# Quarter-sized second-projection operands and earlier requests for kept products in a two-layer hybrid trunk

## The chip, the cores and the metric

The kernel runs on one core of a Trainium2 chip, in one launch. The metric is the device time of that launch in microseconds (us). The kernel before has been run three times: 2802.8, 2805.24 and 2806.19 us, median 2805.24 us. One more execution, of 2806.7 us, was recorded by the profiler; its trace has a span of 2804.9 us, so 1.8 us of that execution lie outside the span.

## The reference

One step of a decoder trunk with two layers is computed for a prompt of 1024 tokens and eight single-token samples, width 1024. Each layer is a token mixer (a gated linear recurrence with a short convolution in layer 0, a state-space mixer in layer 1) and then a squared-ReLU MLP:

```
h = rmsnorm(x, norm_mlp[l]) * (1.0 + s2) + sh2
x = x + g2 * (jnp.square(jax.nn.relu(h @ mlp_w1[l])) @ mlp_w2[l])
```

`mlp_w1` is 1024 x 4096 and `mlp_w2` is 4096 x 1024. Shift, scale and gate (`sh2`, `s2`, `g2`) come from a projection of a condition vector (the "ada" weights). The change lies in these two MLPs alone. Mixers, states and the final norm are computed as before.

## The kernel before

**Layout.** Activations lie transposed: features on the 128 partitions, 1032 columns (1024 tokens and 8 samples) in two halves of 516 (`HX`). Each fp32 value is split into a high part (`fp32r`, a ScalarE cast) and a low part (what is left, a VectorE subtraction), and each product is made of three matmuls, high x high, high x low, low x high (`mm3`, L487; the matmuls are L490, L493 and L494).

**Two-by-two block products.** Both projections are computed block-wise with seven products in place of eight (a fast matrix multiplication scheme), so sums and differences of blocks are formed of weights, inputs and results.

**First projection** (the loop over `AOPS`, L865). The 32 tiles of hidden features make 16 pairs `p`. For each pair there are seven products `q`; each is 24 matmuls of 258 columns into one of four PSUM buffers `pd`. Products 1 and 2 of the first eight pairs (`LEAD`) and of the last four (`TAIL`, pairs 12 to 15) are computed ahead of the others, in a row. Product 1 of such a pair is spilled to DRAM (`keep`, L896) and so is the finished block of product 2 (`B`, L806). They are fetched again when the pair's product 6 comes: `kept` (L856) requests product 1 into half of a `t6` buffer (four of these; weight sums use them too), and L886 requests the block into its slot. Product 6 is evicted by L899, a VectorE subtraction that reads the fetched product 1. The order around the last pairs is: products 1 and 2 of pairs 12, 13, 14, 15, then 6, 7, 5, 4, 3 of pair 12, and so on.

**Between the projections.** Hidden blocks and their sums go to DRAM under seven names (`td`), each as two halves of eight pairs.

**Second projection** (the loop over `BOPS`, L939). Seven products `i`; each has eight steps `j`. A step takes one quarter `q` of the pairs (four pairs) and one half `mp` of the output tiles, 48 matmuls. In the first product the quarters come as 0, 1, 0, 1, 2, 3, 2, 3; in the others as 0, 1, 2, 3, 0, 1, 2, 3. In the last product the steps are halved by columns. After each step the weights of three steps on are prepared (`prepare`, L972): loads on SP's queue into two `raw` buffers and, for four of the products, a second load and a sum or difference in a `t6` buffer (L451, L453, L455), two of them with a store for later; then a cast (L456) and a subtraction (L457). While layer 0's second projection runs, the "ada" weights of layer 1 are loaded and multiplied between the steps (L308, L320).

**Operands of the second projection.** `load_op(i, kh)` (L833) fetches half `kh` of product `i`'s operand: it takes two buffers of one tag, one for the eight high parts and one for the eight low parts. It issues four DMAs of 516 KB on GpSimd's queue (`dma_aux`, L225, kept in program order) into the low buffer, and leaves a list of four parts, each a cast (L843) and a subtraction (L844) over two pairs. `split_op(n)` (L850) issues the next `n` parts. Three sets of two buffers rotate (`BSET`). From product 2 on, the second half of product i+1 is requested after step 5 and the first half of product i+2 after step 7 (L978 to L981), and the parts are issued after the steps by the list `(2, 1, 1, 1, 1, 1, 0, 1)`: of the four parts of a product's second half, one after step 7 of the product before it, two after its own step 0 and one after its step 1. Quarter 2 is first used in step 2 and quarter 3 in step 3.

**What sets the order.** Each engine works through its own list in order. A scheduler makes the lists from the program's order and priorities; instructions that are "kept in program order" stay in it on their engine. GpSimd does nothing but issue DMAs in these stages.

Of the kernel before, what the change touches and what calls it, by code (L numbers as in the profile page):

```python
# [161 lines left out]
def kernel(ctx: ExitStack, tc: tile.TileContext, A: dict):  # L162
# [62 lines left out]
    def dma_aux(out, in_):  # L225

        tc.keep_in_program_order(nc.gpsimd.dma_start(out=out, in_=in_))  # L227
# [557 lines left out]
    def mlp(l, gi, finish, more=None):  # L785
# [7 lines left out]
        def slot(p, i):  # L793
            s = (7 * p + i) % 8
            return M["X"][:, 4 + s // 2, s % 2 * HX:s % 2 * HX + HX]
# [34 lines left out]

        R, todo = {}, []

        def load_op(i, kh):  # L833

            pool, tag = ((big, M["tags"][0]), (ph.pool, "hr"), (big, M["tags"][1]))[BSET[i][kh]]
            ts = [pool.tile([P, KT * 520], F32R, name="rr", tag=tag, bufs=2) for _ in range(2)]
            hi, lo = R[i, kh] = [t[:, 0:KT * HX].rearrange("p (k t) -> p k t", t=HX) for t in ts]
            d = td[BOPND[BPROD[i]]][kh]

            def parts():  # L840
                for c in range(0, KT, 2):
                    src = lo[:, c:c + 2].bitcast(F32)
                    tc.keep_in_program_order(S.copy(hi[:, c:c + 2], src))  # L843
                    V.tensor_sub(lo[:, c:c + 2], src, hi[:, c:c + 2].bitcast(F32))  # L844
                    yield
            for c in range(0, KT, 2):
                dma_aux(lo[:, c:c + 2].bitcast(F32), d[:, c:c + 2])
            todo.append(parts())

# [15 lines left out]
        for i, (p, q) in enumerate(AOPS):  # L865
            n = APOS[p, q]
            while len(got) <= n // 2:
                got.append(need(f"a{l}", len(got), AHEAD - 1))
            if i == 0:
                bg.drain(hgen.pop(3, None))  # L870
                sg = bg.add(mlp_sums())
                bg.step(sg)
            elif i == 2 * LEAD:
                bg.drain(hgen.pop(2), sg)
                sg = bg.add(mlp_more_sums())
            elif i == 2 * LEAD + 4:
                bg.drain(sg)
            if i == 2 * LEAD - 4:
                kept(0)
                kept(1)  # L880
            if q == 6:
                kept(p)
                if p and p + 1 in keep:
                    kept(p + 1)
            if p in SPLIT and q == (5 if p < 2 else 6):
                dma_aux(slot(p, 1), B[p])  # L886
            w = 512 * (n % 2), got[n // 2]
            pt = pd()
            product(w, q, pt)
            pv = pt[:, :, 0:HX // 2]  # L890
            if q == 1:
                U[p, 1] = t2(HX)
                S.copy(v2(U[p, 1]), pv)
                if p in SPLIT:
                    keep[p] = dr.tile([P, HX], F32, name="kept", tag=f"kept{p}")
                    dma_aux(keep[p], U[p, 1])  # L896
            elif q == 6:
                U[p, 1], U[p, 2] = saved.pop(p, U[p, 1]), t2(HX)
                V.tensor_sub(v2(U[p, 2]), v2(U[p, 1]), pv)  # L899
            elif q == 7:  # L900
                U[p, 3] = t2(HX)
                V.tensor_add(v2(U[p, 3]), pv, v2(U[p, 2]))
            elif q == 5:
                c = t2(HX)
                V.tensor_add(v2(c), pv, v2(U[p, 3]))
                V.tensor_add(v2(U[p, 2]), pv, v2(U[p, 2]))
                ff_out(p, q, c, -1.0)
            elif q == 2:
                c = t2(HX) if p in SPLIT else U[p, 1]
                V.tensor_add(v2(c), pv, v2(U[p, 1]))  # L910
                ff_out(p, q, c, 1.0)
            elif q == 4:
                c = U[p, 3] if p < NPAIR - 1 else t2(HX)
                V.tensor_add(v2(c), pv, v2(U[p, 3]))
                ff_out(p, q, c, -1.0)
            else:
                V.tensor_add(v2(U[p, 2]), pv, v2(U[p, 2]))
                ff_out(p, q, U[p, 2], 1.0)
            if n % 2:
                prepare(wpos[0] - 1 + AHEAD)  # L920
            if (p, q) == FRONT[1][-1]:
                load_op(0, 0)
            elif p == NPAIR - 2 and q in (7, 5, 4, 3):
                split_op()
            if (p, q) == (NPAIR - 1, 5):
                split_op(4)
                load_op(0, 1)
            bg.tick(2)

        x = new_x()  # L930
        for m in range(KT):
            dma_aux(x[:, m, :], xd[:, m])
        load_op(1, 0)
        acc = tp.tile([P, KT, NS], F32, name="racc", tag="racc", bufs=2)
        V.memset(acc, 0.0)
        fin = finish()
# [2 lines left out]
        for n, (i, hb, q, mp) in enumerate(BOPS):  # L939
# [3 lines left out]
                ada[0] = more()  # L943
            elif i == 6 and hb == 0 and j == 0:
                ada_steps(99)
            rh, rl = R[i, q // 2]
            seq = BSEQ if i else BFIRST
            qs = [qq for qq, mm in seq if mm == mp]
            for m in (2 * mp, 2 * mp + 1):
                if q == qs[0]:  # L950
                    pts[m] = pd()
                pt = pts[m]
                for b in range(2) if hb is None else (hb,):
                    c = slice(b * hw, b * hw + hw)
                    mm3(pt[:, b, 0:hw], [(hi[:, o:o + P], lo[:, o:o + P], rh[:, k, c], rl[:, k, c])
                                         for k, o in ((q % 2 * 4 + k, 256 * k + m % 2 * P) for k in range(4))],
                        q == qs[0], q == qs[-1])
                if q == qs[-1]:
                    for o, th in BOUT[BPROD[i]]:
                        mt = 4 * o + m  # L960
                        gate = mod[:, gi + mt, 0:1]
                        if hb is None:
                            xv = v2(x[:, mt, th * HX:th * HX + HX])
                            V.scalar_tensor_tensor(xv, pt[:, :, 0:hw], gate, xv, op0=ALU.mult, op1=ALU.add)
                        else:
                            xv = x[:, mt, th * HX + hb * hw:th * HX + hb * hw + hw]
                            V.scalar_tensor_tensor(xv, pt[:, hb, 0:hw], gate, xv, op0=ALU.mult, op1=ALU.add)
                        if hb != 1:
                            sv = pt[:, 0, 0:4] if th else pt[:, 1, hw - 4:hw]
                            av = acc[:, mt, 4 * th:4 * th + 4]  # L970
                            V.tensor_add(av, sv, av)
            prepare(wpos[0] - 1 + AHEAD)  # L972

            if i == 0:
                split_op((0, 2, 2, 0, 1, 1, 2, 0)[j])
            else:
                split_op((2, 2, 1, 1, 1, 1, 0, 1)[j] if i == 1 else (2, 1, 1, 1, 1, 1, 0, 1)[j] if i < 6 else (2, 1, 0, 0, 0, 0, 0, 0)[j] if hb == 0 else 0)
            if j == (5 if i else 3) and i < 6:  # L978
                load_op(i + 1, 1)
            elif j == 7 and i < 5:  # L980
                load_op(i + 2, 0)  # L981

            if i == 6 and j == 7 and hb == 0:
                V.tensor_mul(acc, acc, mod[:, gi:gi + KT, 1:9])
# [1143 lines left out]
```

## Time and profile before

| | |
|---|---|
| median of 3 runs | 2805.24 us |
| profiled execution | 2806.7 us, span 2804.9 us |
| TensorE matmul busy | 2654.7 us (95%), 19442 matmuls |
| VectorE busy | 1983.5 us (71%) |
| ScalarE busy | 1485.0 us (53%) |
| GpSimd busy | 266.5 us (10%) |
| moved by DMA | 525.63 MB |
| mean granted TensorE clock | 0.977 |

The profile is a page on one execution: busy time per engine, a strip of forty time slices, DMA queues, the chain of waits that ended last, and groups of instructions by source line. Behind it stands the trace, which can be asked for waits (who waited for whom), for the instructions of one engine in order of time, and for tables over chosen windows. `out<-in` names the tiles that an instruction writes and reads, L844 is a source line, and a bracket at the end of a timeline row tells how long the engine was idle before it and what released it. Matmuls overlap in the trace, so the spacing of their starts tells the rate, not the busy time of one. The first MLP's two projections run from about 560 to 883 us and from 883 to 1260 us of the span, the second's from about 2120 to 2444 us and from 2444 to 2793 us.

### The profile page before, as it was taken

The page shows a single profiled execution, that of the slowest core. Times are in us where ns is not written, and L with a number is a line of the kernel's source. Part 1 is how long each engine was busy: PE and PEld are TensorE (multiplying, and loading weights), DVE is VectorE, ACT ScalarE, POOL GpSimd, SP SyncE. Part 2 cuts the span into 40 slices and gives each one's busy share as a digit, 9 for nine tenths or more (in the row PEclk, how much of TensorE's full clock was granted, in tenths as well). Part 3 has the DMA queues.
Part 4 walks back from the last instruction along what each step waited for, and adds up shares of the span by engine and source line. Part 5 has one row for each costly group of instructions (what it writes and reads, how often), then busy time and mean ns, then how long its engine had stood idle before and what let it go on. Part 6 is the DMA issues. An engine that isn't in the chain of part 4 may idle for free. (4 is left out here: it accounts for less than half of the span.)

```text
span 2804.9 us, 49250 instructions
## 1 busy us (share of the span) xinstructions
PE 2654.7 (95%) x19442; PEld 2443.9 (87%) x19442; DVE 1983.5 (71%) x3668; ACT 1485.0 (53%) x2409; POOL 266.5 (10%) x492
## 2 busy tenths in 40 slices
PE   6999999999999988998899999999999999999897
PEld 4889888899999977898789897787779999999897
DVE  5666544788757555775789788998778776756676
ACT  5785511464444322356687767878756445433234
POOL 0000000023223100000000000000001322311000
PEclk9999999999999999999899999999999999999998
DMA  8232333257468899834545745444435655779764
GB/s 300 69 107 71 105 121 113 88 191 242 168 204 312 328 334 353 321 129 115 142 148 144 184 122 155 132 132 124 117 105 172 223 184 181 264 284 372 266 214 156
DMA packets 199256, 525.63 MB, mean 187 GB/s; under 512 B 32688, under 2 KB 50736, under 8 KB 199024
## 3 DMA queue, kind: packets, MB, share of 16 engines
q1 hardware_dynamic: 150640, 355.25, 40.3%
q0 software_dynamic: 48384, 167.23, 16.2%
q8 instruction: 153, 2.51, 0.4%
q14 instruction: 79, 0.65, 0.1%
HBM read 408.59 MB, written 113.80 MB: 186 GB/s over the span
## 5 line engine op out<-in xcount | busy, mean ns | idle before, releaser
L490 PE MATMUL pg<-hh,whi 128*128 128x256 f32 (+2 forms) x1616 | 535.8, 332 | 13.5 <-ACT hh L592 6.2
L493 PE MATMUL pd<-rr,whi 128*128 128x258 f32 x1792 | 512.3, 286 | 25.1 <-DVE rr L844 24.9
L493 PE MATMUL pg<-hl,whi 128*128 128x256 f32 (+2 forms) x1616 | 522.8, 324 | 1.9 <-DVE hl L593 1.9
L494 PE MATMUL pg<-hh,wlo 128*128 128x256 f32 (+2 forms) x1616 | 522.0, 323 | 0.0
L490 PE MATMUL pd<-rr,whi 128*128 128x258 f32 x1792 | 513.4, 287 | 0.0
L494 PE MATMUL pd<-rr,wlo 128*128 128x258 f32 x1792 | 510.5, 285 | 1.5 <-DVE wlo L467 1.1
L467 DVE TENSOR_TENSOR wlo<-raw,whi 128x1024 fp32r<-128x1024 f32 x222 | 270.7, 1221 | 216.5 <-ACT whi L466 209.9
L466 ACT CAST whi<-raw 128x1024 fp32r<-128x1024 f32 x222 | 231.4, 1044 | 349.4 <-PE pg L493 192.0
L493 PEld LDWEIGHTS pd<-rr,whi 128*128 128x128 f32 x1792 | 343.6, 192 | 29.2 <-DVE rr L844 27.0
L490 PEld LDWEIGHTS pd<-rr,whi 128*128 128x128 f32 x1792 | 343.7, 192 | 19.0 <-issue 16.5
L490 PEld LDWEIGHTS pg<-hh,whi 128*128 128x128 f32 x1616 | 308.0, 191 | 50.0 <-issue 8.8
L494 PEld LDWEIGHTS pd<-rr,wlo 128*128 128x128 f32 x1792 | 344.0, 192 | 4.0 <-DVE wlo L467 1.8
L493 PEld LDWEIGHTS pg<-hl,whi 128*128 128x128 f32 x1616 | 308.1, 191 | 31.1 <-issue 5.8
L494 PEld LDWEIGHTS pg<-hh,wlo 128*128 128x128 f32 x1616 | 307.4, 190 | 24.4 <-issue 0.7
L490 PE MATMUL pd<-hh,whi 128*128 128x258 f32 x1024 | 293.9, 287 | 18.6 <-DVE t L899 12.6
L493 PE MATMUL pd<-hh,whi 128*128 128x258 f32 x1024 | 292.7, 286 | 0.8 <-DVE hh L695 0.8
L494 PE MATMUL pd<-hh,wlo 128*128 128x258 f32 x1024 | 291.1, 284 | 0.0
L490 PEld LDWEIGHTS pd<-hh,whi 128*128 128x128 f32 x1024 | 196.8, 192 | 21.0 <-issue 13.6
L456 ACT CAST whi<-t 128x1024 fp32r<-128x1024 f32 x64 | 67.0, 1047 | 274.8 <-PE pd L493 116.8
L493 PEld LDWEIGHTS pd<-hh,whi 128*128 128x128 f32 x1024 | 196.3, 192 | 1.9 <-DVE hh L695 1.4
L494 PEld LDWEIGHTS pd<-hh,wlo 128*128 128x128 f32 x1024 | 196.6, 192 | 0.0
L490 PE MATMUL pg<-ffh,whi 128*128 128x264 f32 (+2 forms) x544 | 176.8, 325 | 2.1 <-ACT bcz L1633 1.5
(335 smaller groups left out, 5813.9 us busy)
## 6 DMA issues: line engine op xcount, KB each, us to landing
raw<-W SPq DMA_DIRECT2D x375, 512.0 KB, 4.3
td<-x POOLq DMA_DIRECT2D x224, 258.0 KB, 3.6
rr<-td POOLq DMA_DIRECT2D x112, 516.0 KB, 8.1
t<-ada SPq DMA_DIRECT2D x192, 256.0 KB, 5.4
t<-W SPq DMA_DIRECT2D x32, 512.0 KB, 5.8
sd<-t SPq DMA_DIRECT2D x32, 512.0 KB, 5.8
t<-sd SPq DMA_DIRECT2D x32, 512.0 KB, 5.5
t<-csd SPq DMA_DIRECT2D x64, 256.0 KB, 4.6
```

Source lines behind the costliest of these rows:

```text
L456: S.copy(hi, h)
L466: S.copy(hi, raw)
L467: V.tensor_sub(lo, raw, hi.bitcast(F32))
L490: mm = PE.matmul(pt, wh, xh, start=first and i == 0, stop=False)
L493: PE.matmul(pt, wh, xl, start=False, stop=False)
L494: PE.matmul(pt, wl, xh, start=False, stop=last and i == n - 1)
```

## The change

The operand of a second-projection product comes in four quarters instead of two halves. A quarter takes one buffer, with its four high parts ahead and its four low parts behind; it is requested by two DMAs of 516 KB and has two parts. A buffer is free for the next quarter when that quarter's last step is done, so requests go out after steps 4, 5, 6 and 7 (in the first product after 2, 3, 6 and 7), one quarter each. The parts are issued by the list `(1, 1, 1, 1, 1, 1, 0, 2)` from product 2 on: both parts of quarter 2 after step 7 of the product before, the parts of quarter 3 after steps 0 and 1. The count of DMAs, their sizes, the casts, the subtractions and the matmuls stay as they are.

In the first projection, the kept products of pairs 12 and 13 and the block of pair 12 are requested ahead of product 1 of pair 15, two products ahead of product 6 of pair 12, where they were requested before.

```
-        def load_op(i, kh):
-
-            pool, tag = ((big, M["tags"][0]), (ph.pool, "hr"), (big, M["tags"][1]))[BSET[i][kh]]
-            ts = [pool.tile([P, KT * 520], F32R, name="rr", tag=tag, bufs=2) for _ in range(2)]
-            hi, lo = R[i, kh] = [t[:, 0:KT * HX].rearrange("p (k t) -> p k t", t=HX) for t in ts]
-            d = td[BOPND[BPROD[i]]][kh]
+        def load_op(i, q):
+
+            pool, tag = ((big, M["tags"][0]), (ph.pool, "hr"), (big, M["tags"][1]))[BSET[i][q // 2]]
+            t = pool.tile([P, KT * 520], F32R, name="rr", tag=tag, bufs=2)
+            hi, lo = R[i, q] = [t[:, j * 4 * HX:(j + 1) * 4 * HX].rearrange("p (k t) -> p k t", t=HX)
+                                for j in range(2)]
+            d = td[BOPND[BPROD[i]]][q // 2][:, q % 2 * 4:q % 2 * 4 + 4]
 
             def parts():
-                for c in range(0, KT, 2):
+                for c in range(0, 4, 2):
                     src = lo[:, c:c + 2].bitcast(F32)
                     tc.keep_in_program_order(S.copy(hi[:, c:c + 2], src))
                     V.tensor_sub(lo[:, c:c + 2], src, hi[:, c:c + 2].bitcast(F32))
                     yield
-            for c in range(0, KT, 2):
+            for c in range(0, 4, 2):
                 dma_aux(lo[:, c:c + 2].bitcast(F32), d[:, c:c + 2])
             todo.append(parts())
...
-            if p in SPLIT and q == (5 if p < 2 else 6):
+            if p in SPLIT and q == (5 if p < 2 else 6) and p != NPAIR - TAIL:
                 dma_aux(slot(p, 1), B[p])
+            elif (p, q) == (NPAIR - 1, 1):
+                kept(NPAIR - TAIL)
+                kept(NPAIR - TAIL + 1)
+                dma_aux(slot(NPAIR - TAIL, 1), B[NPAIR - TAIL])
...
             if (p, q) == FRONT[1][-1]:
                 load_op(0, 0)
+                load_op(0, 1)
...
             if (p, q) == (NPAIR - 1, 5):
                 split_op(4)
-                load_op(0, 1)
+                load_op(0, 2)
+                load_op(0, 3)
...
         load_op(1, 0)
+        load_op(1, 1)
...
-            rh, rl = R[i, q // 2]
+            rh, rl = R[i, q]
...
-                                         for k, o in ((q % 2 * 4 + k, 256 * k + m % 2 * P) for k in range(4))],
+                                         for k, o in ((k, 256 * k + m % 2 * P) for k in range(4))],
...
-            if i == 0:
-                split_op((0, 2, 2, 0, 1, 1, 2, 0)[j])
-            else:
-                split_op((2, 2, 1, 1, 1, 1, 0, 1)[j] if i == 1 else (2, 1, 1, 1, 1, 1, 0, 1)[j] if i < 6 else (2, 1, 0, 0, 0, 0, 0, 0)[j] if hb == 0 else 0)
-            if j == (5 if i else 3) and i < 6:
-                load_op(i + 1, 1)
-            elif j == 7 and i < 5:
-                load_op(i + 2, 0)
+            split_op(((0, 2, 1, 1, 1, 1, 1, 1), (2, 2, 1, 1, 1, 1, 0, 2), (1, 1, 0, 0, 0, 0, 0, 0))[2 if i == 6 else i][j]
+                     if i in (0, 1, 6) else (1, 1, 1, 1, 1, 1, 0, 2)[j])
+            at = (4, 5, 6, 7) if i else (2, 3, 6, 7)
+            if j in at and i < 6 and i + 1 + at.index(j) // 2 < 7:
+                load_op(i + 1 + at.index(j) // 2, (2, 3, 0, 1)[at.index(j)])
```

## Prediction

> **What bounds the kernel now.** I read the page first, then TensorE's waits in order of size, then the timeline of TensorE at the ends of the waits that the edits can touch, then the queues behind each of them. From the page and from the list of waits (engine and line, what it waited for, us in total, times, longest):
>
> ```profile
> span 2804.9 us, 49250 instructions
> ...
> PE 2654.7 (95%) x19442; PEld 2443.9 (87%) x19442; DVE 1983.5 (71%) x3668; ACT 1485.0 (53%) x2409; POOL 266.5 (10%) x492
> ```
>
> ```profile
> PE pd L493 <- DVE rr L844: 24.9, 7, 7.4
> ...
> PE pd L490 <- DVE t L899: 12.6, 3, 6.6
> ```
>
> TensorE is busy for 95% of the span, and no matmul is added or removed. So the change can only move time in which TensorE stands still. Two groups belong to it: 24.9 us for the low parts of second-projection operands (L844) and 12.6 us for the eviction that reads a kept product (L899). These are the matmuls that ended those waits; the bracket is the wait:
>
> ```profile
> 835.37 0.55 PE L490 MATMUL pd<-hh,whi 128*128 128x258 f32 x1 [5.29 <-DVE t L899]
> ```
> ```profile
> 1005.31 0.58 PE L493 MATMUL pd<-rr,whi 128*128 128x258 f32 x1 [7.40 <-DVE rr L844]
> ```
> ```profile
> 1187.85 0.58 PE L493 MATMUL pd<-rr,whi 128*128 128x258 f32 x1 [5.03 <-DVE rr L844]
> ```
> ```profile
> 2396.69 0.55 PE L490 MATMUL pd<-hh,whi 128*128 128x258 f32 x1 [6.56 <-DVE t L899]
> ```
> ```profile
> 2550.71 0.39 PE L493 MATMUL pd<-rr,whi 128*128 128x258 f32 x1 [2.06 <-DVE rr L844]
> ```
> ```profile
> 2604.58 0.58 PE L493 MATMUL pd<-rr,whi 128*128 128x258 f32 x1 [7.11 <-DVE rr L844]
> ```
> ```profile
> 2654.30 0.39 PE L493 MATMUL pd<-rr,whi 128*128 128x258 f32 x1 [1.86 <-DVE rr L844]
> ```
> ```profile
> 2661.46 0.39 PE L493 MATMUL pd<-rr,whi 128*128 128x258 f32 x1 [1.16 <-DVE rr L844]
> ```
>
> A long wait costs more than itself. The table of windows (window, its length, busy time and matmuls of TensorE, then the other engines, granted clock, DMA share, GB/s) just after the five longest, and one of undisturbed work:
>
> ```profile
> 835.30:840.20 4.90, 4.83 (x23) 4.87 (x24) 3.53 (x6) 2.44 (x4) 0.55 (x1) 0.51 0.37 107
> ...
> 2396.70:2400.10 3.40, 3.40 (x16) 3.40 (x17) 3.40 (x6) 1.08 (x2) 0.00 (x0) 0.51 0.50 151
> ...
> 1005.30:1010.80 5.50, 5.49 (x25) 5.49 (x26) 5.07 (x7) 0.00 (x0) 0.00 (x0) 0.50 0.89 308
> ...
> 1187.90:1191.70 3.80, 3.80 (x18) 3.80 (x19) 3.31 (x3) 0.00 (x0) 0.00 (x0) 0.50 0.58 189
> ...
> 2604.60:2608.20 3.60, 3.60 (x17) 3.60 (x18) 3.35 (x3) 0.00 (x0) 0.00 (x0) 0.50 0.95 303
> ```
> ```profile
> 2612.00:2640.00 28.00, 28.00 (x236) 28.00 (x235) 17.67 (x24) 8.40 (x9) 2.08 (x4) 1.00 0.71 245
> ```
>
> Undisturbed, a matmul takes 28.00/236 = 0.119 us, so a step of 48 takes 5.7 us. After a wait of 5 us or more the granted clock is one half for a while. The 23 matmuls of 835.30 to 840.20 needed 4.90 us and not 2.74, so 2.2 us went; in the same way 1.5 at 2396.7, 2.5 at 1005.3, 1.7 at 1187.9 and 1.6 at 2604.6.
>
> **Part 1: kept products asked for earlier.** GpSimd's queue and VectorE around the first of the two waits, and the usual time of such a fetch from the list of DMA issues (count, KB, median us to landing):
>
> ```profile
> 816.61 0.54 POOL L227 DMA_DIRECT2D kept<-t  x1 [0.70 <-ACT t L893]
> 823.01 0.54 POOL L227 DMA_DIRECT2D b<-t  x1 [5.86 <-ACT t L804]
> 823.54 2.12 POOL L227 DMA_DIRECT2D rr<-td  x4
> 825.65 1.08 POOL L227 DMA_DIRECT2D t<-kept  x2
> ```
>
> ```profile
> 834.53 0.69 DVE L899 TENSOR_TENSOR t<-t,pd 128x516 f32<-128x516 f32 x1 [6.94 <-DMA t<-kept]
> ```
> ```profile
> t<-kept POOLq DMA_DIRECT2D x24, 258.0 KB, 4.2
> ```
>
> The fetch for pair 12 is issued at 825.65, behind the four 516 KB loads of the next stage's operand, and VectorE gets it at 834.53, 8.9 us later where the median is 4.2. After the edit it stands ahead of the spill of pair 15's product 1, so at about 816.6 on GpSimd's queue. Even with the 8.9 us it would land at 825.5, and with 4.2 at 821. VectorE had stood idle for 6.94 us at 834.53, so since 827.6; the fetch is there first. The three moved issues take 3 x 0.54 = 1.6 us of GpSimd ahead of two stores (816.61, 823.01) and the operand loads, and GpSimd stood idle for 5.86 us before 823.01, which hides them. The requests need a `t6` buffer earlier. Of the four, pair 12's weight sums hold two and pair 13's will take one, so one is free; if it were not, GpSimd's queue would stand with both stores behind it (a rival below). Next in line after L899 are the evictions of products 7 and 5, which wait for nothing fetched. I take both waits and their slow stretches as gone: 5.29 + 2.2 + 6.56 + 1.5 = 15.6 us. Bounds: 0 if the buffer is missing, 16.3 with the 0.7 us of the third L899 wait (12.6 - 5.29 - 6.56).
>
> **Part 2: operands by quarters.** Count what moves. DMAs, casts and subtractions stay as many and as large. Of a product's four late parts, the first (quarter 2, first half) stays after step 7 and the last two (quarter 3) stay after steps 0 and 1; only the second half of quarter 2 moves, from after step 0 to after step 7. This is VectorE at the largest wait, product 3 of layer 1, and the matmul that began its step 2:
>
> ```profile
> 2594.77 1.22 DVE L844 TENSOR_TENSOR rr<-rr 128x1032 fp32r<-128x1032 f32 x1
> ...
> 2601.03 1.23 DVE L455 TENSOR_TENSOR t<-t,raw 128x1024 f32<-128x1024 f32 x1 [1.24 <-DMA t<-sd]
> 2602.17 1.22 DVE L457 TENSOR_TENSOR wlo<-t,whi 128x1024 fp32r<-128x1024 f32 x1
> 2603.30 2.37 DVE L844 TENSOR_TENSOR rr<-rr 128x1032 fp32r<-128x1032 f32 x2
> 2605.59 1.22 DVE L457 TENSOR_TENSOR wlo<-t,whi 128x1024 fp32r<-128x1024 f32 x1
> 2606.73 1.23 DVE L844 TENSOR_TENSOR rr<-rr 128x1032 fp32r<-128x1032 f32 x1
> ```
> ```profile
> 2596.48 0.28 PE L490 MATMUL pd<-rr,whi 128*128 128x258 f32 x1
> ```
>
> Step 2 begins at 2596.48 and stops 0.99 us on (2604.58 - 7.11), at the second half of quarter 2, whose part is the first of the two at 2603.30. That part stood behind two weight sums that waited for transfers. After the edit it follows the part at 2594.77 and ends by 2597.2, so step 2 does not wait. But the last part, quarter 3's second half, keeps its place behind the same sums. Pulled up by the one part that left (2.37/2, some 1.14 us), it ends at 2606.73 + 1.23 - 1.14 = 2606.8. Step 3 would need it one step and six matmuls after 2596.48: at + 5.7 + 0.7 = 2602.9. So a wait of 3.9 us stays where 7.11 + 1.6 was: gain 4.8. The same sum for the other places, where step 2 began 0.99 us before the wait:
>
> ```profile
> 1189.99 1.22 DVE L844 TENSOR_TENSOR rr<-rr 128x1032 fp32r<-128x1032 f32 x1
> ```
> ```profile
> 1008.80 1.23 DVE L844 TENSOR_TENSOR rr<-rr 128x1032 fp32r<-128x1032 f32 x1
> ```
> ```profile
> 2553.99 1.22 DVE L844 TENSOR_TENSOR rr<-rr 128x1032 fp32r<-128x1032 f32 x1
> ```
> ```profile
> 2657.90 1.23 DVE L455 TENSOR_TENSOR t<-t,raw 128x1024 f32<-128x1024 f32 x1 [1.37 <-DMA t<-W]
> ...
> 2660.18 1.23 DVE L844 TENSOR_TENSOR rr<-rr 128x1032 fp32r<-128x1032 f32 x1
> ```
>
> - Layer 0, wait ended at 1187.85: step 2 began at 1181.8, need at 1188.2, ready at 1189.99 + 1.22 - 1.14 = 1190.1. Cost 1.9 for 5.03 + 1.7, gain 4.8.
> - Layer 1, 2550.71: began 2547.7, need 2554.1, ready 2554.1 to 2555.2. Cost about 0.5 for 2.06, gain 1.6.
> - Layer 1, 2654.30 and 2661.46: began 2651.4, need 2657.8, ready 2661.4 (a transfer's wait stands ahead, so nothing is pulled up). Cost 3.6 for 1.86 + 1.16: loss 0.6.
> - Layer 0, 1005.31: began 996.9, need 1003.3, ready 1008.9. Cost 5.6 for 7.40 + 2.5: 4.3. Here the next layer's "ada" weights are loaded as well, and transfers fill the stretch:
>
> ```profile
> 930.00:1141.00 211.00, 192.22 (x1497) 167.25 (x1499) 119.11 (x158) 56.13 (x57) 14.46 (x28) 0.94 0.93 338
> ```
>
> With DMA busy for 0.93 of 211 us, time won is partly waited for again at the next load. I keep half, 2.1.
>
> Sum so far: 4.8 + 4.8 + 1.6 - 0.6 + 2.1 = 12.7 us.
>
> The requests also go out more evenly, one quarter after each of steps 4 to 7 instead of four DMAs after step 5 and four after step 7. What such a burst does to a weight load on SP's queue, in the 8 us before and the 8 us after the one at 2628:
>
> ```profile
> t<-W SPq DMA_DIRECT2D x2, 512.0 KB, 4.0
> ```
> ```profile
> t<-W SPq DMA_DIRECT2D x1, 512.0 KB, 9.4
> ```
>
> Beside the burst the load takes 5.4 us more. The loads that the sums ahead of quarter 3 wait for are issued behind the burst of step 7, which is halved, so they may come up to 2.7 us earlier. I take 1 us at each of the three longer remaining waits outside the "ada" stretch (1188, 2602, 2658): 3 us. From below, 0 (the first half of the burst only moves ahead of them); from above, all that is left of those waits.
>
> On these bursts the Trainium skill, "DMA: Bandwidth & Descriptors" (Queues, rings and completion order), says that each DMA engine takes turns, packet by packet, between the queue rows that have work. By that rule the loads keep their turn beside a burst of any length, a thinner burst gives nothing as long as some of it is running, and the sum would lose the 3 us; the 9.4 us of the trace are more than the double of 4.0 that taking turns would give, so the trace does not settle it.
>
> A second unknown is the half clock after the waits that stay, 3.6 to 5.6 us long: waits of 5.03 us and more had it, those of 2.06 us and less not. As each falls into two pieces (first and second half of quarter 3) I count none; at 1.6 each for three of them it would be 4.8 us, which goes into the range.
>
> Total: 15.6 + 12.7 + 3 = 31.3 us. The profiled execution took 2806.7 us, 1.5 above the median of the runs; so about 2775.4 for such an execution and **2774 us** for the median.
>
> **The rivals.**
> - A: the evener requests cure the sums' waits, and nothing waits at quarter 3. All L844 waits and their slow stretches go: 24.9 + 2.5 + 1.7 + 1.6 = 30.7, with part 1 46.3 us, 2759. For it: 4.0 against 9.4 us. Against it: the brackets at 2601.03 and 2657.90 name loads that are issued only when VectorE gives a buffer free. Chance 0.17.
> - B: the second projections are bound by their transfers, and what is won at step 2 is waited for later. Part 1 alone: 2789.6. For it the 0.93 above, against it the 0.71 of 2612 to 2640. Chance 0.17.
> - C: the early requests do not come early, since a `t6` buffer is missing; part 2 alone, 15.7 us: 2789.5. Chance 0.06. With B as well, no change: 0.04.
> - D, slower: quarter 3's second half becomes late at each of the ten product boundaries. Its part stands behind a later step's weight sum, and VectorE reaches it when that sum's load has come. At the price of the worst row, 3.6 us and a restart at half clock of 1.6, ten are 52 us against the 46.3 that can go at most: 2811. It decides from 4.6 us per boundary on. Against it: four of the ten show no wait now. Chance 0.04.
>
> **How the numbers follow.** The forecast has 0.52. A measurement of this kernel can tell 0.2%, 5.6 us, from no change. The forecast, A, B and C alone are faster by more: 0.92; B with C is the same, 0.04; D slower, 0.04. The range reaches from A to a little beyond B and C: 2759 to 2791; it leaves out D, B with C, and the outer half of A.
>
> **What would show it.** In the changed profile: no DMA wait ahead of L899 near 827 and 2388, and `t<-kept` issued ahead of the four `rr<-td`; no TensorE wait six matmuls into step 2; waits of 1 to 5 us early in step 3 on L844 at the same products; half-clock windows down from five to at most three. Wrong would be L899 waits of the old length, step 2 waits that stay, or new waits on "ada" loads that eat the gain.

## The result, and the profile after

| | before | after |
|---|---|---|
| median of 4 runs | 2805.72 us | 2783.45 us |
| lowest to highest | 2802.8 to 2807.12 us | 2778.73 to 2786.11 us |
| ratio, 95% interval | | 0.992, 0.9902 to 0.9938 |
| profiled execution | 2806.7 us, span 2804.9 us | 2780.9 us, span 2779.1 us |

The changed kernel is faster by 22.3 us, where 31.3 was forecast: inside the range, but 9 us short. In the experiments below one execution, of the kernel with the parts first, took 11362 us and is left out of its ratio. The page of the changed kernel first, with the line on busy time:

```profile
span 2779.1 us, 49295 instructions
...
PE 2650.0 (95%) x19442; PEld 2441.8 (88%) x19442; DVE 1984.7 (71%) x3668; ACT 1485.7 (53%) x2409; POOL 266.2 (10%) x492
```

As expected the matmuls are as many as before, 19442, and so are the instructions on this line of the other engines. What changed is idle time. TensorE's waits in the changed kernel (what waited, what for, us in total, times, longest); lines behind 844 have moved by one to five, so that the eviction L899 is L904 now and the subtraction L844 is L845:

```profile
PE pd L493 <- DVE rr L845: 17.0, 7, 4.1
...
PE pd L320 <- DMA t<-ada: 10.1, 7, 2.3
...
PE pd L494 <- DVE wlo L457: 2.7, 1, 2.7
...
PE pd L490 <- DVE t L904: 1.0, 1, 1.0
```

The wait for the kept product fell from 12.6 to 1.0 us. The wait for second-projection operands fell only from 24.9 to 17.0 us, still in seven pieces, and a wait for second-projection weights (L457) of 2.7 us is new.

Where the time went, by stage. The stages are cut in the traces at the first matmul of each (before the change at 540.96, 883.51, 2108.47 and 2444.21 us, in the changed kernel at 543.24, 878.20, 2088.95 and 2416.02 us) and at the last one of each second projection (before at 1273.88 and 2793.14 us). The rounder times given further above for the kernel before are up to 20 us off these cuts.

| us | first proj., layer 0 | second proj., layer 0 | first proj., layer 1 | second proj., layer 1 |
|---|---|---|---|---|
| before | 342.6 | 390.4 | 335.7 | 348.9 |
| after | 335.0 | 382.9 | 327.1 | 351.3 |
| difference | -7.6 | -7.5 | -8.6 | +2.4 |

The four add up to 21.3 us less; the remaining 4.5 us between the two profiles lie in the mixers, which no edit touches. These differ by that much from one execution to the next: the mixer of layer 1 took 827.9 us in this profile of the changed kernel and 840.3 us in another of the same kernel.

**Part 1, seen in the queue.** GpSimd's queue in the changed kernel, at the place of the first wait:

```profile
818.22 1.07 POOL L227 DMA_DIRECT2D t<-kept  x2
819.28 0.54 POOL L227 DMA_DIRECT2D x<-b  x1
...
825.44 2.11 POOL L227 DMA_DIRECT2D rr<-td  x4
```

The two fetches and the block now go out ahead of the operand loads. VectorE's eviction of product 6 finds its data:

```profile
826.20 0.68 DVE L904 TENSOR_TENSOR t<-t,pd 128x516 f32<-128x516 f32 x1
```

It has no bracket: VectorE did not wait ahead of it. Before the change it waited 6.94 us there.

**Part 2, seen at TensorE.** The matmuls of the changed kernel that ended a wait for second-projection operands or weights, except those under 1 us and one of 2.28 us at 1242.01, on the weights (L467) of layer 0's last product, where 1.11 us were waited before:

```profile
1004.22 0.39 PE L493 MATMUL pd<-rr,whi 128*128 128x258 f32 x1 [3.42 <-DVE rr L845]
...
1179.99 0.58 PE L493 MATMUL pd<-rr,whi 128*128 128x258 f32 x1 [3.71 <-DVE rr L845]
...
2570.44 0.58 PE L493 MATMUL pd<-rr,whi 128*128 128x258 f32 x1 [3.52 <-DVE rr L845]
...
2616.24 0.39 PE L494 MATMUL pd<-rr,wlo 128*128 128x258 f32 x1 [2.70 <-DVE wlo L457]
2634.27 0.58 PE L493 MATMUL pd<-rr,whi 128*128 128x258 f32 x1 [4.14 <-DVE rr L845]
```

By their place among the matmuls of the stage these are: layer 0, product 2 step 3; layer 0, product 5 step 3; layer 1, product 3, the second matmul of step 2, the first that takes a low part; layer 1, product 4 step 1; and product 4 step 3. Three of the five are where the forecast had them. The third one is a step too early, and the fourth is on weights, which the forecast did not have at all.

The windows just after these five, to the end of the slow stretch or beyond it (window, its length, busy time and count of TensorE, weight loads, VectorE, ScalarE, GpSimd, granted clock, DMA share, GB/s):

```profile
1004.20:1009.20 5.00, 4.99 (x29) 4.99 (x30) 2.58 (x4) 0.00 (x0) 0.00 (x0) 0.66 0.90 290
...
1180.00:1184.00 4.00, 4.00 (x21) 4.00 (x22) 2.45 (x3) 0.00 (x0) 0.00 (x0) 0.59 0.11 46
...
2570.40:2575.90 5.50, 5.46 (x25) 5.46 (x26) 5.50 (x5) 0.00 (x0) 0.00 (x0) 0.50 0.68 222
...
2616.20:2620.30 4.10, 4.05 (x21) 4.06 (x22) 4.10 (x11) 0.00 (x0) 0.00 (x0) 0.58 0.79 249
2634.20:2640.00 5.80, 5.73 (x36) 5.73 (x37) 2.15 (x3) 0.00 (x0) 0.00 (x0) 0.73 0.34 129
```

Waits of 2.70 to 4.14 us were each followed by a clock of 0.50 to 0.73. At 0.119 us a matmul the five windows hold work for 3.5, 2.5, 3.0, 2.5 and 4.3 us, so 1.5, 1.5, 2.5, 1.6 and 1.5 us were lost, 8.6 together. A sixth slow stretch of the changed kernel followed a wait of 2.29 us for "ada" weights, which ended at 1043.09:

```profile
1043.10:1046.80 3.70, 3.70 (x17) 2.15 (x18) 2.30 (x8) 0.00 (x0) 0.00 (x0) 0.54 1.02 413
```

It lost 1.7 us (17 matmuls of 0.119 us in 3.70 us). The wait of 2.28 us at 1242.01, of the same length, was followed by full clock. The Trainium skill, "TensorE: Matmul & The Clock Gate" (Part 1: The HAM clock gate), puts the clock down after at least one idle window of about 3.4 us and says that the window runs freely. The trace agrees for the waits of 3.42 us and more; the waits of 2.70 and 2.29 us are shorter than that window and were followed by 0.58 and 0.54 all the same.

### The profile page after: what moved, and what is told of

Its sections match the earlier page's. It is cut to its first block, busy times and chain, and to the rows that moved or that the text cites. A ratio compares the mean times of both kernels' runs of the same rounds, so it can differ in the third digit from the quotient of the medians.

```text
span 2779.1 us, 49295 instructions
## 1 busy us (share of the span) xinstructions
PE 2650.0 (95%) x19442; PEld 2441.8 (88%) x19442; DVE 1984.7 (71%) x3668; ACT 1485.7 (53%) x2409; POOL 266.2 (10%) x492
## 3 DMA queue, kind: packets, MB, share of 16 engines
q8 instruction: 153, 2.51, 0.4%
## 5 line engine op out<-in xcount | busy, mean ns | idle before, releaser
L467 DVE TENSOR_TENSOR wlo<-raw,whi 128x1024 fp32r<-128x1024 f32 x222 | 271.1, 1223 | 219.4 <-ACT whi L466 210.2
L490 PEld LDWEIGHTS pg<-hh,whi 128*128 128x128 f32 x1616 | 309.0, 191 | 49.0 <-issue 11.2
```

The costliest lines, as they stand in the source:

```text
L467: V.tensor_sub(lo, raw, hi.bitcast(F32))
L490: mm = PE.matmul(pt, wh, xh, start=first and i == 0, stop=False)
```

## The experiments

Two explanations of the waits that stayed were set against each other. The *order* explanation: an operand's last parts are ready to be split, but they stand on VectorE's list behind sums of weights (L451, L453, L455) which wait for a load. The *transfer* explanation: the operand or the weights themselves come too late, and a better order only moves the wait. A third question came up on the way, what the stores of the weight sums cost. The kernel before took 2819.64, 2817.25 and 2815.2 us in the three series of runs, each on another chip, so every kernel is told by its ratio to it, with the 95% interval.

**Each part alone.** The kernel before with the earlier requests only:

```
-            if p in SPLIT and q == (5 if p < 2 else 6):
+            if p in SPLIT and q == (5 if p < 2 else 6) and p != NPAIR - TAIL:
                 dma_aux(slot(p, 1), B[p])
+            elif (p, q) == (NPAIR - 1, 1):
+                kept(NPAIR - TAIL)
+                kept(NPAIR - TAIL + 1)
+                dma_aux(slot(NPAIR - TAIL, 1), B[NPAIR - TAIL])
```

> Only the earlier requests for the kept products; the second projections' operands come by halves as before. My account of the changed kernel by stages: the first projections lost 7.6 and 8.6 us, the second ones 7.5 us in layer 0 and gained 2.4 us in layer 1, and 4.4 us went in parts that the diff does not touch. Theory 1 (the two edits are independent, and nearly all of the lasting gain is part 1): 2790 us, 15 to 17 below the kernel before, no wait on L899 over 1 us, the L844 waits of 24.9 us still there. Rival (the first projections' gain is partly waited for again in the second): 2794 to 2800.

Measured: 0.9933 (0.9914 to 0.9953), that is 19 us. Its waits for operands:

```profile
PE pd L493 <- DVE rr L844: 28.9, 9, 7.1
```

And the changed kernel with the earlier requests undone:

```
-            if p in SPLIT and q == (5 if p < 2 else 6) and p != NPAIR - TAIL:
+            if p in SPLIT and q == (5 if p < 2 else 6):
                 dma_aux(slot(p, 1), B[p])
-            elif (p, q) == (NPAIR - 1, 1):
-                kept(NPAIR - TAIL)
-                kept(NPAIR - TAIL + 1)
-                dma_aux(slot(NPAIR - TAIL, 1), B[NPAIR - TAIL])
```

> Only the quarters, with the kept products asked for late as before. Theory 1: 5 to 7 us below the kernel before (2799 to 2801), the two L899 waits of 5.3 and 6.6 us still there, waits on the operand's low parts 17 us in total as in the changed kernel. Rival (quarters alone give the 15.7 us of the forecast, and the two edits hinder one another): 2790.

Measured: 0.9964 (0.9949 to 0.9979), 10 us. Its waits:

```profile
PE pd L493 <- DVE rr L845: 16.6, 10, 4.2
...
PE pd L490 <- DVE t L900: 11.3, 2, 5.9
```

The wait for the kept product is back to 11.3 us (L900 is the same eviction), so part 1 is what takes it away. In the profiles of all the kernels here that have the earlier requests the two first projections took 660.0 to 666.0 us together, against 678.3 before and 680.6 here. The earlier requests alone give about as much as the whole change does (0.9933 against 0.992). The two parts' gains, 19 and 10 us, add up to more than the whole, by about what the intervals leave open.

**The changed kernel again**, in the second series:

> The changed kernel once more, beside the others on one chip, since the kernel before took 2805.7 us in one series and 2819.6 us in another. Both theories: its ratio to the kernel before is again 0.990 to 0.994.

Measured: 0.993 (0.9912 to 0.9948); the first measurement gave 0.992. Its second projections took 389.4 and 348.5 us, 1.4 less than before the change together. So with 5.1 in the first profile and 8.9 in the one without part 1 (383.1 and 347.3), part 2 is worth between 1 and 9 us in these three profiles; by its own runs, 10 us with an interval of 6 to 14.

**The position of the moved part.** The changed kernel with the parts issued as before the change, quarter 2's second part again after step 0:

```
-            split_op(((0, 2, 1, 1, 1, 1, 1, 1), (2, 2, 1, 1, 1, 1, 0, 2), (1, 1, 0, 0, 0, 0, 0, 0))[2 if i == 6 else i][j]
-                     if i in (0, 1, 6) else (1, 1, 1, 1, 1, 1, 0, 2)[j])
+            split_op(((0, 2, 1, 1, 1, 1, 1, 1), (2, 2, 1, 1, 1, 1, 0, 1), (2, 1, 0, 0, 0, 0, 0, 0))[2 if i == 6 else i][j]
+                     if i in (0, 1, 6) else (2, 1, 1, 1, 1, 1, 0, 1)[j])
```

> The changed kernel, but the parts are issued by the list of before: quarter 2's second half after step 0 again. Requests stay spread over steps 4 to 7. Theory 2 (what is left is order on VectorE: parts stand behind weight sums that wait for loads): quarter 2's second half is late again in step 2 at the places of before, 4 to 10 us slower than the changed kernel, 2788 to 2794. Rival (transfers bind the second projections, and a part's place does not matter): within 3 us of the changed kernel, 2781 to 2786.

Measured: 0.9922 (0.9902 to 0.9942), the same as with the part moved. At three of the places of before the waits stood in step 2 again (4.0, 5.0 and 4.0 us), as the order explanation had it; the 4 to 10 us more that it had expected did not come, since the waits add up to nearly the same:

```profile
PE pd L493 <- DVE rr L845: 19.4, 8, 5.0
```

The step that the prediction built part 2 on, moving one of four parts, is worth nothing that these runs can tell. The starts of the products show why. In layer 1, products 3 and 4 took 55.5 and 49.5 us before, 52.3 and 56.3 with the part moved, and 57.1 and 49.0 with it moved back; a product without any wait takes 8 x 5.76 = 46.1. The wait went from product 3 to product 4 and back.

**The order of VectorE's list.** If the parts only stand behind the sums, it is enough to issue them first. Two lines change places:

```
-            prepare(wpos[0] - 1 + AHEAD)
-
             split_op(((0, 2, 1, 1, 1, 1, 1, 1), (2, 2, 1, 1, 1, 1, 0, 2), (1, 1, 0, 0, 0, 0, 0, 0))[2 if i == 6 else i][j]
                      if i in (0, 1, 6) else (1, 1, 1, 1, 1, 1, 0, 2)[j])
+            prepare(wpos[0] - 1 + AHEAD)
```

> The changed kernel with one line moved: the parts of a step are issued ahead of the preparation of the weights of three steps on, so they stand ahead of the newest weight sum and cast on VectorE and ScalarE. Transfers are the same. Theory 2 (order on VectorE): TensorE's wait for operand parts falls from 17.0 us to under 5, and the kernel comes to 2762 to 2772. Rival (transfers bind): the waits go over to the weights (L457) and the ada loads (L320), total within 5 us of the changed kernel, 2779 to 2786.

> The quarters with the parts ahead of the preparation of the weights, again, as the measure for the other three on this chip. Ratio to the kernel before 0.982 to 0.987, no TensorE wait on L845 over 1 us.

Measured: 0.9839 (0.9817 to 0.9861) and, in the third series, 0.9875 (0.9855 to 0.9895). TensorE's waits in the first of the two:

```profile
PE pd L320 <- DMA t<-ada: 10.9, 7, 3.5
...
PE pd L494 <- DVE wlo L457: 7.0, 4, 4.2
PE pd L490 <- DVE racc L979: 4.3, 1, 4.3
```

No wait for `rr` is left, of 17.0 us, and the two second projections took 721.2 and 715.1 us in the two profiles, against 734.2 and 737.9 in those of the changed kernel. The loads did not come earlier for it: VectorE's waits from 2600 to 2632 us, around product 4 of layer 1, in the changed kernel

```profile
DVE t L455 <- DMA t<-W: 13.2, 3, 6.0
```

and in the one with the parts first:

```profile
DVE t L455 <- DMA t<-W: 15.1, 3, 7.9
```

The sums wait as long as ever, but the operand's parts no longer wait with them. The order explanation is shown, and for the operands the transfer explanation falls. What remains at TensorE are the loads themselves, the "ada" weights (L320) and the sums' own results (L457), and a new wait for an eviction (L979, 4.3 us; 3.4 in the other run), so part of the gain is paid back there.

The other way to the same end leaves the sums ahead and issues three of a product's four late parts one step earlier (after steps 6, 7, 7 and 0 where it was 7, 7, 0 and 1):

```
-            split_op(((0, 2, 1, 1, 1, 1, 1, 1), (2, 2, 1, 1, 1, 1, 0, 2), (1, 1, 0, 0, 0, 0, 0, 0))[2 if i == 6 else i][j]
-                     if i in (0, 1, 6) else (1, 1, 1, 1, 1, 1, 0, 2)[j])
+            split_op(((0, 2, 1, 1, 1, 1, 1, 1), (2, 2, 1, 1, 1, 1, 1, 2), (1, 0, 0, 0, 0, 0, 0, 0))[2 if i == 6 else i][j]
+                     if i in (0, 1, 6) else (1, 0, 1, 1, 1, 1, 1, 2)[j])
```

> The changed kernel with each operand part of the late quarters issued a step earlier: quarter 2's parts after steps 6 and 7, quarter 3's after steps 7 and 0. Weight sums stay ahead of the parts of the same step. Theory 2 (order on VectorE): one step is 5.8 us, more than the waits that are left (4.1 us at most), so TensorE's waits on L845 fall from 17 to under 4 us and the kernel gains 8 to 14 us on the changed one. Rival (transfers bind, the wait only changes its name): within 3 us of the changed kernel.

Measured: 0.9868 (0.984 to 0.9897).

```profile
PE pd L493 <- DVE rr L845: 1.6, 4, 0.5
```

The same gain by another road. Both edits together:

> The quarters, the parts first and each late part a step earlier, both mendings at once. Theory 2 (the order is mended by either, and nothing is left for the other): within 4 us of the run with the parts first alone. Rival (some of its remaining waits, 4.3 us on an eviction and 7.0 us on weights, come from parts that VectorE does in a crowd): 6 to 10 us faster than it.

Measured: 0.9853 (0.9834 to 0.9873). That is 5.5 us less by the medians than the parts first alone in the same series, 0.9875 (0.9855 to 0.9895), but the intervals overlap, so a further gain is not shown; the second projections took 720.8 us, no less than with either edit alone (721.2, 715.1 and 722.3).

**The sums on another engine.** If VectorE's list is the trouble, the sums could leave it. L451, L453 and L455 on GpSimd:

```
-                    V.tensor_add(h, h, raw)
+                    nc.gpsimd.tensor_add(h, h, raw)
...
-                    V.tensor_sub(h, raw, h)
+                    nc.gpsimd.tensor_sub(h, raw, h)
...
-                    V.tensor_sub(h, h, raw)
+                    nc.gpsimd.tensor_sub(h, h, raw)
```

> The changed kernel with the weight sums and differences of the second projections (L451, L453, L455) on GpSimd instead of VectorE; every transfer and the list of parts stay. VectorE then has nothing in its list that waits for a load directly, except through the cast. Theory 2: waits on L845 under 4 us, 8 to 14 us faster than the changed kernel, if a sum of 128 x 1024 takes GpSimd less than a step (5.8 us). Rival (transfers bind): within 3 us of the changed kernel, the waits on the weights (L457) and the ada loads instead. If GpSimd is slow or its operand requests stand behind the sums: 10 us and more slower.

Measured: 1.0005 (0.9991 to 1.002); the whole gain is lost, as the last sentence of the expectation had it. One group of the sums (x count, busy us in total, mean ns, then idle time before them):

```profile
L455 POOL TENSOR_TENSOR t<-t,raw 128x1024 f32<-128x1024 f32 x32 | 78.6, 2461 | 146.4 <-DMA raw<-W 60.2 <-DMA t<-W 33.3 <-DMA t<-sd 22.6
```

A sum takes 2.46 us there, 1.23 on VectorE. And GpSimd's list is not empty: the operand requests (`rr`) stand in it. All of the loss lies in the second projection of layer 1, 379.1 us against 348.5 in the changed kernel of the same series, and there in products 4 and 5, 69.8 and 61.5 us (58.0 and 46.1). GpSimd in product 4, which began at 2613.6, and ScalarE's wait for operand loads in this projection:

```profile
2617.84 2.39 POOL L455 TENSOR_TENSOR t<-t,raw 128x1024 f32<-128x1024 f32 x1 [5.33 <-DMA t<-W]
2620.17 1.09 POOL L227 DMA_DIRECT2D rr<-td  x2
2628.19 4.64 POOL L455 TENSOR_TENSOR t<-t,raw 128x1024 f32<-128x1024 f32 x2 [6.92 <-DMA t<-W]
2632.78 1.09 POOL L227 DMA_DIRECT2D rr<-td  x2
```
```profile
ACT rr L844 <- DMA rr<-td: 18.7, 6, 5.0
```

The requests have no bracket: they went out as soon as the sum ahead of them was done, and the sums waited 5 to 8 us each for their loads. So the operands were loaded late, ScalarE's casts waited 18.7 us for them (4.1 in the first profile of the changed kernel), and TensorE waited for the casts. VectorE's subtractions beside the sums were slower as well (L457 took 1.56 us on average, 1.22 in the changed kernel). The edit moved the sums from one list, where they held up the operand's parts, into another one, where they held up the operand's requests.

**Halves or quarters, once the order is mended.** The kernel with the earlier requests alone, operands by halves, with the parts first:

```
-            prepare(wpos[0] - 1 + AHEAD)
-
             if i == 0:
                 split_op((0, 2, 2, 0, 1, 1, 2, 0)[j])
             else:
                 split_op((2, 2, 1, 1, 1, 1, 0, 1)[j] if i == 1 else (2, 1, 1, 1, 1, 1, 0, 1)[j] if i < 6 else (2, 1, 0, 0, 0, 0, 0, 0)[j] if hb == 0 else 0)
+            prepare(wpos[0] - 1 + AHEAD)
```

> Operands by halves as in the kernel before, kept products asked for early, and the parts issued ahead of the preparation of the weights, as in the run with the parts first. It asks what quarters add once VectorE's order is mended. Theory 2a (the order was all): within 3 us of the run with quarters and the parts first, ratio to before 0.983 to 0.986. Rival (halves come too late for parts that go first, so that the cast or the part waits for its load): waits on the operand parts of 10 us or more, ratio 0.988 to 0.994.

> The halves with the parts first, again, beside the quarters with the parts first. Theory 2a (with VectorE's order mended, quarters add nothing that can be told): within 4 us of it. Rival (quarters are worth the difference of the two series, 0.984 against 0.988): 8 to 14 us slower than it.

Measured: 0.9879 (0.9857 to 0.9901) and 0.9896 (0.9879 to 0.9913). The waits of the first of the two:

```profile
PE pd L320 <- DMA t<-ada: 12.2, 4, 5.5
PE pd L494 <- DVE wlo L457: 9.8, 4, 4.3
```

By halves, too, the operand waits are gone (of 28.9 us 0.3 are left in one run and none in the other). In the third series quarters stand 0.2% better, 0.9875 against 0.9896, or 7.4 us by the medians, between the two expectations, and the intervals overlap. 0.9839 and 0.9879, from different series, point the same way, and the size is not settled. In the profiles the second projections took 731.8 and 735.9 us by halves, against 721.2 and 715.1 by quarters. The order is worth more than the quarters: two lines in the kernel with the earlier requests gain about 0.4 to 0.5%.

**The stores of the weight sums.** Four of the seven products form sums of weights, and two of them store theirs for later. This kernel has the parts first and leaves those stores out; what was read back is replaced by as large a read of other weights, so the sums that two later products need are not formed:

```
-                    sumd[n, q, mp] = sd(n)
-                    sums.append((idx, sumd[n, q, mp], h))
+                    sumd[n, q, mp] = A["W"][WIDX[second]]
```

> The quarters with the parts first, and the stores of the weight sums of products 2 and 3 left out; what is read back of them later is read from the weights instead, as many bytes. So 32 stores of 512 KB go, a wrong operand takes the place of the sums. Theory 3 (with the order mended, what is left in the second projections is loads that come late, held up by the other transfers and by buffers that the stores hold): the waits on L457 and on the ada loads, 7.0 and 10.9 us, fall by half or more, 8 to 12 us faster than with the stores. Rival (the loads are late by their own chain, issue after buffer, one at a time): within 3 us.

Measured: 0.9788 (0.9767 to 0.981) against 0.9875 (0.9855 to 0.9895) with the stores, in the same series: 25 us by the medians. The two profiled executions are only 6.1 us apart (the one with the stores was the fastest of its kernel, the one without the slowest), so the profiles cannot place the 25 us. In them the second projections took 368.9 and 337.3 us against 377.9 and 337.2, 9 us less, all in layer 0. There the "ada" waits go from 11.1 us to

```profile
PE pd L320 <- DMA t<-ada: 0.8, 1, 0.8
```

The waits for the sums' results did not fall (3.2 us with the stores, 4.4 without). The 32 stores are 512 KB each, 16.8 of 525.6 MB; the 16 of layer 0 are issued in the stretch in which the "ada" weights are loaded. So the "ada" waits that stay hang on the stores or on what reads them back. Whether it is the traffic or the place in a list is not shown: stores and "ada" loads stand in one list, SP's, and with the stores, from 930 to 1130 us of the span, that list waited

```profile
SPq L221 <- DMA sd<-t: 56.3, 14, 6.6
```

for a store to land, with the loads behind it; without them this wait is gone, and SP waited more for VectorE in its place (39.6 us for L455 and 38.4 for L457).

## Why the prediction was right, and where it was wrong

- **Part 1, forecast 15.6 us.** Measured 7.6 + 8.6 = 16.2 us in the two first projections; alone, 19 us by its runs, with an interval of about 5 either way. Mechanism and size were right, and the cover named for it (GpSimd idle ahead of the stores) held. The third wait of this group stayed, 1.0 us.
- **Part 2, forecast 12.7 us for the waits and 3 for the bursts.** Measured between 1 and 9 us in three profiles, 10 by the runs of the quarters alone. This is the term that was mis-sized, and it failed at one step: "After the edit it follows the part at 2594.77 and ends by 2597.2, so step 2 does not wait." That took VectorE's list of before and lifted one instruction in it. But the list is made anew. VectorE in the changed kernel, ahead of that step:

```profile
2563.95 1.23 DVE L455 TENSOR_TENSOR t<-t,raw 128x1024 f32<-128x1024 f32 x1 [5.00 <-DMA sd<-t]
...
2568.02 1.22 DVE L457 TENSOR_TENSOR wlo<-t,whi 128x1024 fp32r<-128x1024 f32 x1
2569.15 2.37 DVE L845 TENSOR_TENSOR rr<-rr 128x1032 fp32r<-128x1032 f32 x2
```

Both parts of quarter 2 (2569.15, x2) now stand behind a sum of weights that waited 5.00 us, four evictions and a subtraction, although ScalarE had cast them long before:

```profile
2556.20 2.00 ACT L844 CAST rr<-rr 128x1032 fp32r<-128x1032 f32 x2
```

They were ready to be subtracted at 2558.2, and the subtraction came 11 us later. Before, one of them was late; now both were, and TensorE stopped at the second matmul of step 2 and not at the eighth.

- **By place.** Layer 1, product 3: forecast 4.8 us less, measured 55.5 to 52.3, 3.2 less. Product 2: forecast 1.6, measured 48.3 to 46.9, 1.4. Product 4: forecast 0.6 more, measured 49.5 to 56.3, 6.8 more. Its list:

```profile
2613.83 1.23 DVE L455 TENSOR_TENSOR t<-t,raw 128x1024 f32<-128x1024 f32 x1 [6.04 <-DMA t<-W]
2614.97 1.22 DVE L457 TENSOR_TENSOR wlo<-t,whi 128x1024 fp32r<-128x1024 f32 x1
```

  The sum waited 6.04 us for its load, and the weights of step 1 came 2.70 us late for it; the wait in step 3 was 4.14 us and each had its stretch of half clock. So what had been won in product 3 was paid back in product 4. Layer 0: product 5 was forecast 4.8 less (5.8 with the burst), measured 53.0 to 51.5, 1.5 less; product 2 was forecast 2.1, measured 3.2. Another 8.3 us went from product 3, whose "ada" waits fell from 7.9 to 2.8 us, with most of the half clock behind them, and 3.3 came back in product 4, with 3.0 us of such waits that it did not have. The forecast had nothing there. So its 7.9 for this stage meets the measured 7.5 by a coincidence of terms; in the second profile of the same kernel the stage gained 1.0 us.
- **What the gain of the second projections was made of.** In these two profiles the waits for operands and for sums, with the half clock behind them, went only from 24.9 + 0.3 + 5.8 = 31.0 us to 17.0 + 2.7 + 8.6 = 28.3. The "ada" waits and theirs went from 11.2 + 5.6 = 16.8 us to 10.1 + 1.7 = 11.8. So more of the measured gain came from a place without a forecast than from the one that the sum was made for.
- **The bursts, 3 us.** Not seen at the three waits that they were counted for. The median landing of the sums' second loads, over the whole trace, before

```profile
t<-W SPq DMA_DIRECT2D x32, 512.0 KB, 5.8
```

  and after:

```profile
t<-W SPq DMA_DIRECT2D x32, 512.0 KB, 7.0
```

  They did not come sooner beside thinner bursts, and the 9.4 us of the forecast were the time of a single load; between 5.1 and 8.9 us the median varies over the runs whatever the edit. The rule of taking turns, named in the prediction from the Trainium skill, "DMA: Bandwidth & Descriptors" (Queues, rings and completion order), would have given nothing here, and nothing was found. In the "ada" stretch there may be an effect that the forecast did not look for: products 3 and 4 of layer 0 took 116.4 to 118.2 us together in the four profiles with halves and 113.2 to 116.3 in the eight with quarters that keep the sums on VectorE and store them. What in the quarters does it, the thinner bursts or the buffers that come free in another order, no run separates.
- **The half clock after short waits**, put at none and at 4.8 us at most, cost 8.6 us, and 1.7 more behind an "ada" wait. The forecast said at most three such windows; there are six (without the one at the end of layer 1, which both profiles have). The profile before could have told: the forecast compared waits of 5.03 us and more with those of 2.06 us and less, but three "ada" waits lay between, of 3.31, 2.98 and 4.94 us, and each had its slow stretch:

```profile
1050.90:1055.20 4.30, 4.27 (x22) 3.30 (x23) 1.61 (x6) 0.00 (x0) 0.00 (x0) 0.60 1.03 420
1062.40:1065.40 3.00, 2.99 (x13) 1.33 (x14) 0.00 (x0) 0.00 (x0) 0.00 (x0) 0.50 0.55 195
1111.60:1116.60 5.00, 4.99 (x22) 3.32 (x23) 0.35 (x1) 0.00 (x0) 0.00 (x0) 0.50 1.04 410
```

  By the matmuls in them they lost 1.7, 1.5 and 2.4 us, 5.6 together. So the count of none for waits of 3.6 to 5.6 us had rows against it.
- **The rivals.** A (all operand waits go by themselves) is out: 17.0 us stayed. B (transfers take back what is won) would have given nearly the measured time, 2789.6 against 2783.45, but for the operands not by its mechanism, since the waits go without a transfer becoming faster (parts first). In layer 0 what is left does hang on other transfers, as the kernel without the stores shows, though not whether by their traffic or by their place in SP's list. C is out, because the requests did go early. D, a late quarter at every boundary, did not come; one boundary of the ten got worse by more than its 4.6 us, product 4 of layer 1.
- **Better than both kernels** is the change with the parts issued ahead of the weight sums: 0.9839 and 0.9875 of the time before, where the change as made has 0.992 and 0.993.

## What to carry to other kernels

An engine that works its list in order turns one instruction that waits for a transfer into a wait for all behind it (here parts that were ready 11 us before); so put work whose inputs are there ahead of work that waits for a transfer, and try that before changing sizes or requests. When an edit moves one instruction between others that a scheduler orders, the list after cannot be had by lifting that one instruction in the list before: give such a gain a range that reaches to nothing, and look whether the wait turns up at the next product. When a wait is counted at a price, look at every wait of its length in the profile, not only at those that the edit touches. And two edits that were made together are worth measuring apart: here one of them alone gives 0.9933 where both give 0.992 and 0.993.

## What the runs showed of the hardware

Half clock followed waits as short as 2.29 us in the changed kernel (0.54 in the 3.70 us from 1043.10) and 1.77 us in the second run with the parts first, where one of 1.45 us had ended 7.8 us ahead of it:

```profile
2619.54 0.39 PE L494 MATMUL pd<-rr,wlo 128*128 128x258 f32 x1 [1.77 <-DVE wlo L457]
```
```profile
2619.50:2623.20 3.70, 3.66 (x18) 3.66 (x19) 3.70 (x4) 0.00 (x0) 0.00 (x0) 0.54 0.53 158
```

Yet a wait of 2.28 us in the changed kernel (ended 1242.01) and one of 2.51 us with the parts issued a step earlier (ended 1239.07) had full clock in the 4 us behind them, as had the operand waits up to 2.06 us in the profile before. So between 1.8 and 2.5 us the length of the wait did not decide by itself. A sum of two 128x1024 fp32 tiles took 2.46 us on GpSimd and 1.23 us on VectorE, and GpSimd's DMA requests stood behind sums that waited 5 to 8 us for their loads.
